# A second value/gate pair of a projection computed by seven block products, with moves of three kinds of work around it

## The chip, the cores and the metric

One core of one Trainium2 chip. The time is that of one execution in microseconds of device time, shown as the median of several runs; a profiled execution has a time of its own. The engines are TensorE (PE, with its weight loads PEld), VectorE (DVE), ScalarE (ACT), GpSimd (POOL) and SyncE (SP). SP, ACT and POOL can issue DMA transfers, each from a queue of its own, in order.

## The reference

One layer of a hybrid decoder trunk over 1024 positions of 1024 channels, in float32. Only the first half matters here:

```python
h = rms_norm(x, g_mix[l])
z = jnp.einsum("bsd,de->bse", h, w_in[l]) + b_in[l]
va, ga, xb, gb, sa, sb = jnp.split(z, cuts, axis=-1)      # 1024, 1024, 1536, 1536, 1024, 1024 channels
u = va * jax.nn.sigmoid(ga)
u = causal_depthwise_conv(u, conv_a_w[l], conv_a_b[l])    # width 31; then layer norm, silu, w_a_out -> y_a
v = causal_depthwise_conv(xb, conv_b_w[l], conv_b_b[l])   # width 4
v = rg_lru(v, ...)                                        # two gates by 16 heads of 96 x 96, then a scan
y_b = einsum(v * gelu(gb), w_b_out[l])
m = sigmoid(sa) * y_a + sigmoid(sb) * y_b                 # then w_o, residual, MLP of 4096, residual, norm
```

## The kernel before

Every float32 product is made of three matmuls on split operands: high part by high, high by low, low by high (`mm3`, `chunk_mm`, `z_mm`). A high part is a rounded copy by ACT. A low part is made either by DVE (a subtraction, function `split` or a `later` entry) or through POOL: `split_dma` (lines 63 to 68) lets ACT write the negated rounded value and a DMA issued by POOL add the source onto it.

The input projection has two stages.

**Chunks.** A chunk is 128 output channels over all 1024 positions. List `CH` (line 711) gives their order, three of them begun before the loop. A chunk takes 24 weight blocks by two halves of the positions, 48 matmuls (`chunk_mm`). In each slot of the loop (`for s in range(3, NC1)`) PE runs one chunk, with the two gate products of a head (`head_mm`, six matmuls each, into one PSUM buffer of the tag `ps2`) between its parts, in slots 4 to 23. ACT reads a head's bank with a sigmoid (`head_gate`, line 541); in every group of four heads, the third (head 2, 6, 10, 14) is spread over three tiles, by three row transfers per gate (line 546). After a group of four heads `scan_exp` (exponential and tanh), `scan_root` (square root), `scan_in` and `scan_tile` prepare and run the recurrence of three channel tiles. `VA+j` and `GA+j` are the value and gate chunks of channel tile j of branch A; `NJ` tiles go this way.

**Block products.** The other channels go in pairs of chunks (`ZPAIRS`), each by a Winograd form of Strassen's scheme: seven products of half-size blocks in place of eight. A product (i, p) is 12 matmuls into one PSUM bank (`z_mm`, line 948). `zseq` is the order of all products, a place each. At place n the loop also makes the left operand of place n + 4 (`z_lhs`), the sums of blocks for place n + 5 (`z_sums`), and the work after the products of places n - 1 and n - 2 (`z_post`, `z_post2`). `ZL` says at which place the weights of a pair are loaded, into four buffers of the tag `p`, and `ZX` holds further work by place. Right operands 4 to 7 are sums of blocks of the normed input: computed and stored early (`x_sum`, `x_make`, `x_store`), those in `RAW` unsplit, and fetched back (`x_get` for split parts, `x_raw` then `x_split` for raw ones). The pair `u7` is the last value/gate pair; `z_branch` puts it together.

**What fills DVE.** The width-31 convolution (`conv`) of each of the eight channel tiles of branch A is 48 steps on DVE. The planner keeps clocks of expected time (`clk`) for PE, ACT and DVE; `later` queues a DVE operation with a time when it is ready, `vector_work` emits the queue in that order, and `fill` puts convolution steps into the gaps. While `taps["hold"]` is set no new convolution begins. A convolution's result is stored (`yd`, line 661) and added up by POOL's DMA queue (`sum_up`); the sum is needed in the middle of the following stage, branch B's projection (`b_mm`, with `n_mean`).

Later stages (branch A's output projection `ga`, the projection `go`, the MLP's first products `gu` and `f`) have an order by places too (`gseq`, `GX`); `up_lhs` makes left operands of the MLP.

The order on each engine is the order in which these loops emit, and each engine and queue works in order.

Of the kernel before, what the change touches and what calls it, by code (L numbers as in the profile page):

```python
# [15 lines left out]
P = 128  # L16
# [5 lines left out]
HD = 96  # L22
# [9 lines left out]
def trunk_kernel(ctx: ExitStack, tc: tile.TileContext, x, xt_in, xt_eo, vecs, w_in, w_a_out, w_b_out,  # L32
                 w_rg, w_o, w_1, w_2, g_final, out):

    nc = tc.nc
# [458 lines left out]
    gate = {}  # L494
# [39 lines left out]
    def head_gate(n, gi, ready):  # L534
        g, hh = divmod(n, 4)
        tiles = [3 * g + WHOLE[hh]] if hh in WHOLE else range(3 * g, 3 * g + 3)
        for t in tiles:
            if (gi, t) not in gate:
                gate[gi, t] = T(f"g{gi}_{t}")
        a = gate[gi, tiles[0]][:HD] if hh in WHOLE else H(f"g{n}_{gi}", "g")  # L540
        nc.scalar.activation(a, gps.pop((n, gi))[:HD, :], AF.Sigmoid,  # L541
                             bias=(ba_c, bx_c)[gi][:, n:n + 1])
        at("A", 1.11, ready)
        if hh not in WHOLE:
            for ti, t in enumerate(tiles):
                nc.sync.dma_start(gate[gi, t][HD:P, :], a[32 * ti:32 * ti + 32, :])
# [163 lines left out]
    NJ = 7  # L710
    CH = [XB + 0, VA + 0, GA + 0, XB + 1, XB + 2, VA + 1, GA + 1, XB + 3, XB + 4, XB + 5, VA + 2, GA + 2, XB + 6, XB + 7, XB + 8, VA + 3, GA + 3, XB + 9, XB + 10, XB + 11, VA + 4, GA + 4, VA + 5, GA + 5, GA + 6, VA + 6]
    NC1 = len(CH)
# [25 lines left out]
    def chunk_mm(s, n0, n1, halves=(0, 1), low_last=False):  # L738
# [16 lines left out]
        for t in "s0 s1 g0 g1 g2 s2 s3 u7 g3 g4 g5 t0 t1 t2 t3".split()]  # L755
# [31 lines left out]
    def z_lhs(i, p):  # L787
        src = z_blk(i, *{1: (0, 0), 2: (0, 1), 4: (1, 1)}[p]) if p in (1, 2, 4) else \
            zs[i, {3: 4, 5: 1, 6: 2, 7: 3}[p]]
        zn[0] += 1  # L790
        o = (wp.tile([P, 2, 4, P], F32R, tag="w", name=f"zo{i}_{p}") if zn[0] % 5 > 2 or zn[0] % 5 == 0 else
             qp.tile([P, 2, 4, P], F32R, tag="g", name=f"zo{i}_{p}", bufs=2))
        if p in (7, 5) or conv_over():
            nc.scalar.activation(o[:, 0], src, AF.Copy)
            later(at("A", 0.6), 0.63, nc.vector.tensor_tensor, o[:, 1], src, o[:, 0].bitcast(F32),
                  ALU.subtract)
        else:
            split_dma(src, o[:, 0], o[:, 1])
            at("A", 1.15)
        zo[i, p] = o  # L800


    zseq = [(0, 1), (1, 1), (0, 2), (1, 2), (0, 6), (0, 7), (1, 7), (0, 5), (1, 6), (0, 3), (0, 4),
            (1, 5)]
    for i in range(2, NZ):
        zseq += [(i, 1), (i, 7), (i - 1, 4), (i, 6), (i, 2), (i - 1, 3), (i, 5)]
# [4 lines left out]
    for i in range(2, NZ):  # L811
        n = zseq.index((i, 1))
        ZL[n - 9] = ((z_load, i, 0),)
        ZL[n - (6 if i > 2 else 4)] = ((z_load, i, 1),)
    def z_get(n, f):
# [8 lines left out]
    RAW = (4, 5)  # L824
    XS = {4: ((x_sum, 0),), 5: ((x_make, 0, 5), (x_make, 0, 7)), 6: ((x_make, 0, 6), (x_make, 0, 4), (x_sum, 1)),
          7: tuple((x_make, 1, p) for p in (5, 7, 6, 4)),
          NC1 - 3: ((scan_exp, 3),), NC1 - 2: ((x_get, 0, 6), (x_get, 1, 6)),
          NC1 - 1: ((scan_in, 0, 9, 10, 11), (scan_root, 3), (x_get, 0, 7), (x_get, 1, 7))}
# [204 lines left out]
    def z_post2(i, p):  # L1033
# [3 lines left out]
        elif p == 4:  # L1037
            z_out(i, 1, 0, zb[i, "u"], "c")

    ZX = {0: ((x_raw, 0, 5), (x_raw, 1, 5)), 1: ((later, 0, 4.8, scan_tile, 9),), 2: ((x_split, 0, 5),), 3: ((x_split, 1, 5),),  # L1040
          4: ((later, 0, 4.8, scan_tile, 10), (x_raw, 0, 4), (x_raw, 1, 4)), 6: ((x_split, 0, 4),), 7: ((x_split, 1, 4),),
          9: ((later, 0, 4.8, scan_tile, 11),)}
    H_AT = {2: (0, 0), 5: (1, 1), 3: (0, 1), 4: (1, 0)}
    with tc.manual_schedule(engines=ENGINES):
# [40 lines left out]
        u_value(NJ - 1, zps[NC1 - 1])  # L1085
        vector_work(clk["V"])
        z_h(0, 0, 0)
        for n in range(len(zseq) + 2):
# [5 lines left out]
            taps["hold"] = n < 6  # L1094
# [598 lines left out]
    def g_get(n, f):  # L1693
# [34 lines left out]
        7: ((g_parts, "u", 5, 1), (up_lhs, 1, 5), (g_t, "u", 0, 3), (g_t, "u", 1, 3)),  # L1728
        9: ((g_parts, "u", 7, 0), (up_lhs, 0, 7)), 10: ((g_parts, "u", 7, 1), (up_lhs, 1, 7)),
# [463 lines left out]
```

## Time and profile before

| | us |
|---|---|
| median of 3 runs (1542.11 to 1543.1) | 1542.4 |
| the profiled execution's own time | 1542.07 |
| its span, first to last instruction | 1540.3 |
| granted TensorE clock, mean | 0.998 |
| DVE busy in the span | 1228.9 |
| ACT busy in the span | 911.2 |
| POOL busy in the span | 184.7 |

A line of the profile names an engine, a line of the kernel, the tile written and the tiles read, then times. "busy" is time in which an engine worked; the idle time before an instruction is put down to what released it. PEld is the weight load of TensorE, which runs beside its matmuls.

### The profile page before, as it was taken

How to read it: one execution, taken by the hardware profiler on the slowest of the kernel's cores; microseconds unless marked ns; L12 is line 12 of the kernel's file. 1: busy time of each engine (PE TensorE's matmuls, PEld its weight loads, DVE VectorE, ACT ScalarE, POOL GpSimd, SP SyncE). 2: the span in 40 equal slices, each digit the busy share in tenths (PEclk: the TensorE clock that was granted, in tenths of full speed). 3: DMA queues.
4: the chain of work that ended last, by engine and by line, in shares of the span. 5: the costliest groups of instructions: out<-in, count | busy, mean ns of one | idle time of the engine just before them, and what ended most of it. 6: DMA issues, size and time to landing. Idle time of an engine off the chain costs nothing.

```text
span 1540.3 us, 19049 instructions
## 1 busy us (share of the span) xinstructions
PE 1530.1 (99%) x6765; PEld 1258.2 (82%) x6765; DVE 1228.9 (80%) x1660; ACT 911.2 (59%) x1270; POOL 184.7 (12%) x221
## 2 busy tenths in 40 slices
PE   9999999999999999999999999999999999999998
PEld 7888888788888888888888887888888888888886
DVE  6999988989999998478568879765555558888897
ACT  6758576667676676435375777444444475555553
POOL 0000000012222221000022332000000011111110
PEclk9999999999999999999999999999999999999999
DMA  7575554699998888844579898523333779888852
GB/s 295 115 235 149 149 145 116 159 280 244 255 249 214 219 225 253 272 172 128 187 194 304 191 194 201 195 82 132 114 116 108 241 212 232 223 225 222 204 125 110
DMA packets 133504, 296.02 MB, mean 192 GB/s; under 512 B 20896, under 2 KB 38944, under 8 KB 133408
## 3 DMA queue, kind: packets, MB, share of 16 engines
q1 hardware_dynamic: 102016, 215.10, 41.5%
q0 software_dynamic: 30672, 77.35, 27.5%
q10 hardware_dynamic: 720, 2.36, 0.4%
q8 instruction: 53, 0.87, 0.2%
q14 instruction: 43, 0.35, 0.1%
HBM read 155.03 MB, written 60.82 MB: 140 GB/s over the span
## 4 chain that ended last, share of the span: by engine, by line
PE 97%; DMA 1%; ACT 1%; DVE 1%; issue 0%; SPq 0%; POOL 0%; DVEq 0%; POOLq 0%; ACTq 0%
PE z L749 16%; PE d L1946 15%; PE yb L1165 8%; PE e L2063 3%; PE keep L1946 2%; PE z L257 2%; PE rg L529 1%; PE rg L531 1%; PE rg L530 1%; DMA w_raw<-in_w_dram 1%; DMA xc<-in_xt_dram 0%; PE z4a L948 0%; PE go2e L1341 0%; PE z4e L948 0%; PE z2e L948 0%; PE z3e L948 0%
## 5 line engine op out<-in xcount | busy, mean ns | idle before, releaser
L749 PE MATMUL z<-xh,win_h 128*128 128x512 f32 x368 | 115.0, 390 | 0.0
L1958 DVE TENSOR_TENSOR acc<-acc,d 128x1024 f32<-128x1024 f32 x72 | 87.8, 1220 | 33.4 <-PE d L1946 32.7
L749 PE MATMUL z<-xl,win_h 128*128 128x512 f32 x368 | 113.5, 389 | 0.0
L749 PE MATMUL z<-xh,win_l 128*128 128x512 f32 x368 | 91.8, 391 | 0.0
L653 DVE SCALAR_TENSOR_TENSOR y<-u,vec,y 128x511 f32<-128x511 f32 (+14 forms) x120 | 88.4, 737 | 0.0
L653 DVE SCALAR_TENSOR_TENSOR y<-yt,csum,y 128x511 f32<-128x511 f32 (+6 forms) x112 | 82.6, 738 | 0.0
L653 DVE SCALAR_TENSOR_TENSOR yt<-u,vec,yt 128x511 f32<-128x511 f32 (+6 forms) x112 | 82.6, 737 | 0.0
L749 PEld LDWEIGHTS z<-xh,win_l 128*128 128x128 f32 x368 | 69.1, 188 | 15.6
L749 PEld LDWEIGHTS z<-xh,win_h 128*128 128x128 f32 x368 | 69.0, 188 | 15.3 <-ACT win_h L68 0.4
L541 ACT ACTIVATE g<-rg,vec 96x1024 f32<-96x1024 f32 x32 | 35.7, 1115 | 77.0 <-PE rg L531 76.3
L749 PEld LDWEIGHTS z<-xl,win_h 128*128 128x128 f32 x368 | 69.1, 188 | 14.6
L1623 ACT ACTIVATE o<-s 128x512 fp32r<-128x512 f32 x58 | 34.7, 624 | 54.6 <-DVE s L1608 24.5
L475 DVE SCALAR_TENSOR_TENSOR v<-xb,vec,v 128x1023 f32<-128x1023 f32 (+2 forms) x36 | 46.2, 1283 | 14.8 <-ACT v L466 13.9
L67 POOL DMA_DIRECT2D win_l<-win_raw x23 | 19.9, 867 | 306.9 <-ACT win_l L66 245.7
L67 POOL DMA_DIRECT2D zo<-zw x42 | 36.3, 863 | 130.6 <-ACT zo L66 108.0
L1165 PE MATMUL yb<-hgh,wb_h 128*128 128x512 f32 x168 | 51.7, 389 | 0.0
L1165 PE MATMUL yb<-hgl,wb_h 128*128 128x512 f32 x168 | 51.7, 389 | 0.0
L67 POOL DMA_DIRECT2D db_1l<-wr x7 | 6.1, 865 | 309.9 <-DMA wr<-in_w_dram 254.2
L1165 PE MATMUL yb<-hgh,wb_l 128*128 128x512 f32 x168 | 41.0, 389 | 0.0
L66 ACT ACTIVATE zo<-zw 128x512 fp32r<-128x512 f32 x42 | 26.3, 626 | 21.5 <-issue 6.6
L1129 DVE TENSOR_TENSOR o<-s,o 128x512 fp32r<-128x512 f32 x58 | 38.8, 683 | 0.0
L1172 DVE TENSOR_TENSOR sb<-yb,sb 128x512 f32<-128x512 f32 x16 | 10.3, 685 | 34.4 <-PE yb L1165 34.4
(1826 smaller groups left out, 4750.7 us busy)
## 6 DMA issues: line engine op xcount, KB each, us to landing
w_raw<-in_w_dram SPq DMA_DIRECT2D x36, 512.0 KB, 5.7
fr<-fd SPq DMA_DIRECT2D x32, 512.0 KB, 5.7
wr<-in_w_dram SPq DMA_DIRECT2D x32, 512.0 KB, 6.6
zw<-in_w_in_dram SPq DMA_DIRECT2D x30, 512.0 KB, 6.7
win_raw<-in_w_in_dram SPq DMA_DIRECT2D x23, 512.0 KB, 4.5
win_l<-win_raw POOLq DMA_DIRECT2D x23, 512.0 KB, 4.6
zo<-zw POOLq DMA_DIRECT2D x42, 256.0 KB, 5.9
gates<-zg SPq DMA_DIRECT2D x32, 256.0 KB, 3.8
```

The costliest lines, as they stand in the source:

```text
L67: nc.gpsimd.dma_start(l, src, accum_op=ALU.add)
L257: nc.tensor.matmul(z0[i][:, HALVES[hf]], w0[i][w][:, k, :], xpart(a, hf, k), start=k == 0 and which == "hh", stop=k == 7 and which == ("hl ...
L475: nc.vector.scalar_tensor_tensor(v[:, d:S], a[:, 0:S - d], cbw_c[:, w * 12 + t:w * 12 + t + 1], v[:, d:S], ALU.mult, ALU.add)
L541: nc.scalar.activation(a, gps.pop((n, gi))[:HD, :], AF.Sigmoid, bias=(ba_c, bx_c)[gi][:, n:n + 1])
L653: nc.vector.scalar_tensor_tensor(o[:, k:], a[:, 0:HS - k], c, o[:, k:], ALU.mult, add)
L749: nc.tensor.matmul(zps[s][:, HALVES[hf]], w[:, k, :], xw[k][part][hf], start=n == 0, stop=n == 23)
L1129: tt(l, src, h.bitcast(F32), ALU.subtract)
L1165: nc.tensor.matmul(ps[hf], a, b[:, HALVES[hf]], start=n == 0, stop=n == len(todo) - 1)
L1623: nc.scalar.activation(o[:, 0], src, AF.Copy)
L1946: nc.tensor.matmul(o, a, b, start=n == 0 and (p != 1 or g == 0), stop=n == len(todo) - 1, skip_group_check=p == 1 and g > 0)
L1958: tt(acc[p, q2], acc[p, q2], ps, ALU.add)
L2063: nc.tensor.matmul(o, a, b, start=n == 0 and t < 7, stop=n == len(todo) - 1, skip_group_check=t == 7)
```

## The change

- `NJ` goes from 7 to 6: chunks `GA+6` and `VA+6` leave `CH`, and the order of the last two becomes `GA+5`, `VA+5`. The pair `u6` enters `ZPAIRS` as the seventh of sixteen.
- The products of the first pairs are reordered: (0, 4) goes from place 10 to 15, (1, 4) from 14 to 16, (1, 5) from 11 to 10, (1, 3) from 17 to 13. Pair 3's first weights are loaded seven places ahead of its first product, not nine.
- Right operand 7 is now stored raw, fetched late and split at places 2 and 3; operand 5 is split at 4 and 5, operand 4 at 12 and 13. The last group's exponentials move into the slot of head 14's gates (two tiles) and place 0 (one), its square roots to place 5, its scans to places 6, 8 and 11.
- The first five left operands get their low parts from DVE, not through POOL.
- Head 14's six row transfers are issued by ACT, not SP.
- Holds on new convolutions: the last slot (before: the last three), and places 0 to 4 (before: 0 to 5).
- In the MLP's start `up_lhs` of (1, 5) moves from place 7 to place 9 of its list.

```diff
-                nc.sync.dma_start(gate[gi, t][HD:P, :], a[32 * ti:32 * ti + 32, :])
+                (nc.scalar if n > 11 else nc.sync).dma_start(gate[gi, t][HD:P, :], a[32 * ti:32 * ti + 32, :])
...
-    NJ = 7
+    NJ = 6
...
-        for t in "s0 s1 g0 g1 g2 s2 s3 u7 g3 g4 g5 t0 t1 t2 t3".split()]
+        for t in "s0 s1 g0 g1 g2 s2 u6 s3 g3 u7 g4 g5 t0 t1 t2 t3".split()]
...
-        if p in (7, 5) or conv_over():
+        if p in (7, 5) or zn[0] <= 5 or conv_over():
...
-    zseq = [(0, 1), (1, 1), (0, 2), (1, 2), (0, 6), (0, 7), (1, 7), (0, 5), (1, 6), (0, 3), (0, 4),
-            (1, 5)]
-    for i in range(2, NZ):
+    zseq = [(0, 1), (1, 1), (0, 2), (1, 2), (0, 6), (0, 7), (1, 7), (0, 5), (1, 6), (0, 3), (1, 5)]
+    zseq += [(2, 1), (2, 7), (1, 3), (2, 6), (0, 4), (1, 4), (2, 2), (2, 5)]
+    for i in range(3, NZ):
         zseq += [(i, 1), (i, 7), (i - 1, 4), (i, 6), (i, 2), (i - 1, 3), (i, 5)]
...
-        ZL[n - 9] = ((z_load, i, 0),)
+        ZL[n - (9 if i != 3 else 7)] = ((z_load, i, 0),)
...
-    RAW = (4, 5)
+    RAW = (4, 5, 7)
...
-          NC1 - 3: ((scan_exp, 3),), NC1 - 2: ((x_get, 0, 6), (x_get, 1, 6)),
-          NC1 - 1: ((scan_in, 0, 9, 10, 11), (scan_root, 3), (x_get, 0, 7), (x_get, 1, 7))}
+          NC1 - 2: ((scan_exp, 3, (0, 1)),),
+          NC1 - 1: ((x_get, 0, 6), (x_get, 1, 6), (x_raw, 0, 7), (x_raw, 1, 7), (scan_in, 0, 9, 10))}
...
-            taps["hold"] = s > NC1 - 4
+            taps["hold"] = s in range(23, 99)
...
-    ZX = {0: ((x_raw, 0, 5), (x_raw, 1, 5)), 1: ((later, 0, 4.8, scan_tile, 9),), 2: ((x_split, 0, 5),), 3: ((x_split, 1, 5),),
-          4: ((later, 0, 4.8, scan_tile, 10), (x_raw, 0, 4), (x_raw, 1, 4)), 6: ((x_split, 0, 4),), 7: ((x_split, 1, 4),),
-          9: ((later, 0, 4.8, scan_tile, 11),)}
+    ZX = {2: ((x_split, 0, 7),), 3: ((x_split, 1, 7),), 0: ((scan_exp, 3, (2,)),),
+          4: ((x_split, 0, 5),), 5: ((x_split, 1, 5), (scan_root, 3)),
+          6: ((later, 0, 4.8, scan_tile, 9),), 8: ((x_raw, 0, 4), (x_raw, 1, 4), (later, 0, 4.8, scan_tile, 10)),
+          12: ((x_split, 0, 4),),
+          13: ((x_split, 1, 4),), 11: ((later, 0, 4.8, scan_tile, 11),)}
...
         u_value(NJ - 1, zps[NC1 - 1])
+        scan_in(0, 11)
         vector_work(clk["V"])
+        x_raw(0, 5)
+        x_raw(1, 5)
...
-            taps["hold"] = n < 6
+            taps["hold"] = n in range(0, 5)
...
-        7: ((g_parts, "u", 5, 1), (up_lhs, 1, 5), (g_t, "u", 0, 3), (g_t, "u", 1, 3)),
-        9: ((g_parts, "u", 7, 0), (up_lhs, 0, 7)), 10: ((g_parts, "u", 7, 1), (up_lhs, 1, 7)),
+        7: ((g_parts, "u", 5, 1), (g_t, "u", 0, 3), (g_t, "u", 1, 3)),
+        9: ((up_lhs, 1, 5), (g_parts, "u", 7, 0), (up_lhs, 0, 7)), 10: ((g_parts, "u", 7, 1), (up_lhs, 1, 7)),
```

More of the change, by code (lines that the diff above doesn't have):

```diff
@@ L708, in x_split @@
               ALU.subtract)
-    NJ = 7
-    CH = [XB + 0, VA + 0, GA + 0, XB + 1, XB + 2, VA + 1, GA + 1, XB + 3, XB + 4, XB + 5, VA + 2, GA + 2, XB + 6, XB + 7, XB + 8, VA + 3, GA + 3, XB + 9, XB + 10, XB + 11, VA + 4, GA + 4, VA + 5, GA + 5, GA + 6, VA + 6]
+    NJ = 6
+    CH = [XB + 0, VA + 0, GA + 0, XB + 1, XB + 2, VA + 1, GA + 1, XB + 3, XB + 4, XB + 5, VA + 2, GA + 2, XB + 6, XB + 7, XB + 8, VA + 3, GA + 3, XB + 9, XB + 10, XB + 11, VA + 4, GA + 4, GA + 5, VA + 5]
     NC1 = len(CH)
```

## The prediction, as it was made

> **What bounds the kernel now.** I read the page first: the busy shares, then the chain that ended last. The reader is to see that TensorE (PE) is busy for 99% of the span and owns 97% of the chain, while every other engine has idle time.
>
> ```profile
> span 1540.3 us, 19049 instructions
> PE 1530.1 (99%) x6765; PEld 1258.2 (82%) x6765; DVE 1228.9 (80%) x1660; ACT 911.2 (59%) x1270; POOL 184.7 (12%) x221
> PE 97%; DMA 1%; ACT 1%; DVE 1%; issue 0%; SPq 0%; POOL 0%; DVEq 0%; POOLq 0%; ACTq 0%
> ```
>
> A share is a mean over stages, so next come the windows by stage: the end of the projections by chunks (314 to 339.2 us), and the block products (339.2 to 627). Columns: busy time with count of PE, weight loads, VectorE (DVE), ScalarE (ACT), GpSimd (POOL), granted clock, DMA share, GB/s.
>
> ```profile
> 314.00:339.20 25.20, 25.20 (x111) 20.49 (x110) 21.19 (x30) 22.80 (x25) 4.31 (x5) 1.00 0.91 301
> 339.20:627.00 287.80, 287.80 (x1270) 237.76 (x1269) 262.40 (x388) 195.65 (x320) 62.98 (x73) 1.00 0.91 239
> ```
>
> PE is busy all the time in both. But ACT around the changeover (22.80 of 25.20, 90%) and DVE in the products (91%) are nearly full, so they can take over if more is put on them. Third, all that PE waited for (in total, times, longest), and rows of the chain in order of time (start, length, what) from the chunks and the block products:
>
> ```profile
> PE spare L344 <- POOL ones L114: 1.6, 1, 1.6
> PE gu4a L1341 <- ACT u_late L1395: 0.6, 1, 0.6
> PE z L257 <- ACT xh L226: 0.4, 2, 0.2
> PE z L257 <- DVE xl L230: 0.2, 1, 0.2
> ```
>
> ```profile
> 305.00 8.18 PE z L749 x36
> 339.39 2.72 PE z0a L948 x12
> 624.43 2.72 PE z14f L948 x12
> ```
>
> All waits together are 2.8 us of 1540, and 1.6 of it is before the start of the work. So this kernel is a row of matmuls laid end to end: its time changes by the number of matmuls, plus any wait that a change makes or removes. A product of 12 matmuls takes 2.72 us, 0.2267 us each; 36 take 8.18, the same.
>
> **The change part by part.**
>
> *Matmuls.* A chunk is 24 pairs by two halves, 48 matmuls; chunks VA+6 and GA+6 go, 96 in all, 96 x 0.2267 = 21.76 us. The pair u6 comes in as seven products of 12: 84, 19.04 us. The difference is **-2.72 us**, all of it on the path. Nothing hides it, because PE waits for nobody in these stages.
>
> *One stall goes.* In the chunk stage of before one chunk started late, as its parts stood behind the exponentials on ACT:
>
> ```profile
> 324.43 3.79 PE L749 MATMUL z<-xh,win_l 128*128 128x512 f32 x16
> 328.21 0.73 PE L749 MATMUL z<-xh,win_h 128*128 128x512 f32 x2
> 328.79 0.62 PE L749 MATMUL z<-xl,win_h 128*128 128x512 f32 x2
> ```
>
> 16 x 0.2267 from 324.43 end at 328.06, and the next pair takes 0.73 instead of 0.62: 0.15 + 0.11 = 0.26 us. That chunk was VA+6; in the new kernel the last chunk's parts are made a slot earlier, ahead of the exponentials. **-0.26.**
>
> *ScalarE in the last two slots.* All slots up to 23 keep their place, and the products start at 339.39 - 21.76 - 0.26 = 317.4. What ACT did in two further slots has to fit ahead of that or behind it. The ACT rows of before:
>
> ```profile
> 300.88 1.11 ACT L541 ACTIVATE g<-rg,vec 96x1024 f32<-96x1024 f32 x1 [5.57 <-PE rg L531]
> 302.60 0.71 ACT L636 ACTIVATE yt<-u,vec 128x512 f32<-128x512 f32 x1
> 314.61 1.11 ACT L541 ACTIVATE g<-rg,vec 96x1024 f32<-96x1024 f32 x1 [6.57 <-PE rg L531]
> 315.74 1.28 ACT L556 ACT_TABLE_LOAD   x1
> 317.04 1.16 ACT L556 ACTIVATE a<-g,c 128x1024 f32<-128x1024 f32 x1
> 321.51 1.14 ACT L556 ACTIVATE a<-g,c 128x1024 f32<-128x1024 f32 x1
> ```
>
> ```profile
> L546 SPq DMA_DIRECT2D g<-g x24: 507/542/1143, 95.0 to 303.2; - x24
> L684 ACTq DMA_DIRECT2D xsd<-xs7h x2: 326/336/346, 79.3 to 105.5; - x2
> ```
>
> Behind head 14's second gate (300.88, done 302.0) ACT now also issues three row transfers, then loads the table for the exponentials of two tiles, runs them, and only then comes to the convolution's two copies and head 15's first gate, which needs the sigmoid's table back. Until that gate has read it, head 15's bank (tag ps2, one buffer) stays full, and PE wants it for the head's second product right behind the 36 matmuls of the chunk, at 305.00 + 8.18 = 313.2. This wait is new. Six row transfers on ACT's queue do not appear in before; bounds are 0.34 each (ACT's own issues) and 0.54 (the same rows on SP), with 1.14 the longest. I take 0.54, since that row is of the same shape. The first three fall into ACT's idle 5.57 us and cost nothing. Then: 302.0 + 3 x 0.57 with gaps = 303.7; table 1.30, 305.0; two tiles at 321.51 - 317.04 = 4.47, 309.5; two copies 0.71 each, 310.9; table 1.30, 312.2; gate 1.12, 313.3. PE is held for 0.1 and restarts 0.1 slower, as the late chunk above did; with as much again for the semaphores I take **+0.3** (0 with 0.34 per issue, 2.1 with 1.14). SP, for its part, is rid of the six rows (3.2 us) and gets to the first loads for the products that much sooner. What is late next: two high copies and their lows on DVE are wanted at 317.4 + 0.45 (the third matmul); ACT has them at 314.4, DVE at about 315.8, hidden with 2 us to spare. ACT's own remainder (gate of the values, head 15's second gate, two copies) ends near 317.5, where the products begin, so nothing is queued up.
>
> Here the Trainium skill speaks against the change. Its page "ScalarE: Activation LUTs", section "What ACT_TABLE_LOAD costs", counts a drain of about 1380 ns on top of a load of about 1283, 2.66 us for each switch. The trace disagrees: ACT is done at 315.72, the load runs 315.74 to 317.02 and the next function starts at 317.04. By the page the two new switches would hold PE for some 2.8 us more, an estimate.
>
> *Edits with one answer.* Rows of before, the first a window (columns as above):
>
> ```profile
> 339.40:366.60 27.20, 27.20 (x121) 22.52 (x121) 26.69 (x32) 19.15 (x30) 4.34 (x5) 1.00 0.88 229
> L452 DVE TENSOR_TENSOR zo<-zs,zo x33: 666/685/694, 348.0 to 610.9; 128x512 fp32r<-128x512 f32 x33
> 328.81 3.49 DVE L452 TENSOR_TENSOR g<-g,v 128x1024 f32<-128x1024 f32 x3
> ```
>
> Five lows on DVE instead of POOL: 5 x 0.69 = 3.4 us of DVE, five POOL issues less. DVE was full in the first ten products (26.69 of 27.20) and PE was never held. Into that stretch now come the lows, one product of the scan's input (3.49 / 3 = 1.16) and block 7's two lows of the same size; out of it go block 4's two lows, and the three scans are spread to places 6, 8 and 11. Hidden; if that cover is gone, the 3 us net are PE's. Block 7's raw store takes copies and issues from ACT and DVE in slots 5 to 7, off the path; its raw load is asked for by 314, with a flight of at most 11.5 (row below) it is there at 326, and ACT splits it at places 2 and 3 for place 5, 331. The rest of the new pair's work (four sums, lows, gates' products, some 8 us of DVE) goes into a stage with 16 us more of products than before.
>
> *Products 4 later.* (0,4) goes from place 10 to 15, (1,4) from 14 to 16, so the raw blocks of pairs 0 and 1 that they read are held until places 11 and 12 split them, and pair 3's blocks, which take those buffers, load later. Rows of before:
>
> ```profile
> 368.53 0.32 SPq L577 DMA_DIRECT2D hd<-g  x1
> 368.95 0.38 SPq L764 DMA_DIRECT2D zw<-in_w_in_dram  x1
> zo<-zw POOLq DMA_DIRECT2D x42, 256.0 KB, 5.9
> DMA to landing us min/median/max: 4.2/6.7/11.5
> ```
>
> (The last is that of the zw loads.) Place n starts at 317.4 + 2.72n. The split for (0,4) starts on ACT near 348.1; 0.6 later POOL can issue, and it lands 5.9 after: 354.6. SP has the store of the last scan tile ahead, done about then. Load 354.6, landing at 361.3. ACT wants it for (3,1) at place 15, 358.2, so ACT stands 3 us; (3,1) is split at 361.3 and lands at 367.8, wanted at place 19, 369.1 + 0.45. It decides from a flight of 8.5 us on: bounds 0 and 3.0 us of PE. I take **+0.2**.
>
> *Conversions in the MLP start.* up_lhs(1,5) moves behind two products. PE's 0.6 us wait for u_late stood behind its two copies, 1.0 us (the first of them and what follows):
>
> ```profile
> 946.31 0.62 ACT L66 ACTIVATE o<-s 128x512 fp32r<-128x512 f32 x1
> 947.83 0.58 ACT L1395 ACTIVATE u_late<-gu4a 128x512 f32<-128x512 f32 x1
> 949.85 0.63 ACT L66 ACTIVATE o<-s 128x512 fp32r<-128x512 f32 x1 [0.49 <-DVE s L1611]
> 950.90 0.58 ACT L1395 ACTIVATE u_late<-gu5a 128x512 f32<-128x512 f32 x1
> 951.54 3.01 PE gu5a L1341 x12
> ```
>
> The first u_late comes 1 us sooner. But the second hangs on DVE's s (949.85), which does not move, and gu5a started at 951.54 right behind it; PE only gets there sooner and waits there. Its POOL issue and low land some 1 us later than before, for a product wanted behind gu5a. Taken: **0** (bounds -1.0, both waits gone with their slow restarts, and +0.3).
>
> *Tail of the convolutions.* The last two channel tiles of branch A now come from places 53 and 74, 462 and 519 us, and their taps fill what DVE has left. Rows of before: the last convolution's store, the last add into ysum, and the split that needs it.
>
> ```profile
> L661 SPq DMA_DIRECT2D yd<-y x8: 320/364/1214, 128.9 to 595.7; - x8
> L614 POOL DMA_DIRECT2D ysum<-yd x7: 871/1225/1258, 409.8 to 598.8; - x7
> L1203 ACT ACTIVATE ysumh<-ysum x1: 1044/1044/1044, 642.4 to 642.4; 128x1024 fp32r<-128x1024 f32 x1
> ```
>
> Some 8 us more work on an engine that is 91% full, and 2.5 us less time up to there: 11 of the 43 us between 598.8 and 642.4. **0.**
>
> **Sum**: -2.72 - 0.26 + 0.3 + 0.2 + 0 = **-2.5 us**. The profiled execution took 1542.07 (span 1540.3 and 1.8 around it): 1539.6. The median shown is 0.3 above it, so I give **1539.9**.
>
> **The rivals.**
> A (forecast), 1539.3 to 1541: as above.
> B, every new wait is hidden and the MLP waits go: -2.72 - 0.26 - 1.0 = -4.0, so 1538.4 to 1539.3. For it: two of my waits are within 0.3 us of none. Against: gu5a hangs on DVE.
> C, ScalarE becomes the bound at head 15's bank: the three issues at 1.14 add 1.8 us, or each switch of table takes twice its 1.28 us, 2.6 more: 1541 to 1542.6. For it: ACT is full from 302 to 317. Against: the rows at 315.74 and 317.04, ACT's own issues of 0.34. The table rule has 0.03 of the chance (the skill's page above is where it stands).
> D, **slower**: pair 3's blocks come late. If both fly near the longest, 11.5, the first holds (3,1) by 3.0 us and the second, asked for at 358, lands at 369.5 where DVE wants it for its sums at place 17, 363.7; DVE then stands for 5.8 us, and behind it in order the adds that empty banks, taken as half of that for PE. -2.5 - 0.2 + 3.0 + 2.9 = +3.2, 1545.6; with the spread 1542.6 to 1547. It decides from a flight of 8.5 us on and is slower than before from about 11. Against: the median flight is 6.7.
> That the pair is not really cheaper is excluded: 84 matmuls against 96 is a count.
>
> **How the numbers follow.** Chances: A 0.40, B 0.27, C 0.15, D 0.18. A measurement of this kernel can tell about 0.2%, 3.1 us, from no change. Over 0.2% faster is below 1539.3, case B: 0.27. Over 0.2% slower is above 1545.5, most of D: 0.13. The rest, 0.60, lies within. Range 1538.2 to 1545.0: below B's end nothing, above it a little over D's 0.13.
>
> **What would show it.** PE count 6753; products from 317.7 to about 622.5; a PE wait for ACT g (L541) near 313 of 0 to 0.5 us; no slow pair in the last chunk; ACT standing some 3 us for zw near 358; gu5a with the wait that gu4a had; last yd store near 595. The prediction is wrong if PE waits for zo's lows at places 0 to 10, if any PE wait is over 1 us, or if the product's 2.72 us changes.

## The result, and the profile after

| | before | after |
|---|---|---|
| median of the runs side by side, us | 1542.75 (1542.11 to 1543.65, 4 runs) | 1556.34 (1553.12 to 1557.4, 4 runs) |
| ratio after to before, 95% interval | | 1.0084 (1.0067 to 1.0102) |
| profiled execution, its span | 1542.07, 1540.3 | 1553.12, 1551.3 |

In what follows the *rows* are head 14's six row transfers, *lefts* are left operands of the block products, *lows* their low parts, *raw blocks* the stored right operands that are split late, and a *bank* is the PSUM buffer that a product or a gate is added up in. "After" is the changed kernel.

The change makes the kernel 13.6 us slower; 1539.9 was forecast, with a range up to 1545.0. The profiled execution of after is the fastest of its four, so its trace holds 11.0 us of the difference, not 13.6.

First the page of after: span, busy times, and the chain by engine.

```profile
span 1551.3 us, 19074 instructions
PE 1531.0 (99%) x6753; PEld 1257.0 (81%) x6753; DVE 1234.4 (80%) x1668; ACT 924.3 (60%) x1291; POOL 188.0 (12%) x225
PE 91%; DMA 4%; issue 2%; DVE 1%; ACT 1%; SPq 0%; POOL 0%; DVEq 0%; POOLq 0%
```

The 12 matmuls fewer are there (6765 to 6753). DVE and ACT do 5 and 13 us more, nothing that a span of 1551 could not hold. But PE's share of the chain falls from 97 to 91%, and DMA, DVE and ACT come in: the row of matmuls now has holes. All that PE waited for in after (in total, times, longest):

```profile
PE z0a L948 <- ACT z0b L1014: 3.5, 1, 3.5
PE yb L1170 <- ACT hgh L1070: 1.7, 1, 1.7
PE spare L344 <- POOL ones L114: 1.6, 1, 1.6
PE gu4a L1346 <- ACT u_late L1400: 1.2, 1, 1.2
PE z0f L948 <- DVE xb4l L452: 1.1, 2, 0.7
PE z2e L948 <- DMA zo<-zs: 0.7, 1, 0.7
...
PE rg L529 <- ACT g L541: 0.3, 1, 0.3
```

A wait also makes the next matmuls slower (the first distance behind one is mostly 0.34 us), so I count holes by the starts of successive matmuls: the sum of what each distance has beyond 0.227 us, of the distances over 0.245 and from 45 us on. That gives 2.16 us in before and 16.18 in after, 14.0 more; less 2.72 for the 12 matmuls it is 11.3, and the spans differ by 11.0. The holes account for the whole loss. By place: head 15's bank at 313.0, 0.59; place 2 of the block products at 326.5, 5.35; places 13 to 30 (358 to 410 us), 4.64; one at 524, 0.50; the start of the second projection (644 to 646), 2.80; gu4a and gu5a 1.84 (1.17 before).

How the largest came about is read on three engines. DVE, then ACT, then PE of after (start, length, what, and in brackets the idle time before it with what ended it):

```profile
303.67 0.75 DVE L653 SCALAR_TENSOR_TENSOR y<-yt,csum,y 128x510 f32<-128x510 f32 x1
307.99 2.36 DVE L452 TENSOR_TENSOR g<-g,v 128x1024 f32<-128x1024 f32 x2 [3.57 <-DMA g<-g]
...
315.11 1.27 DVE L452 TENSOR_TENSOR zo<-zw,zo 128x512 fp32r<-128x512 f32 x2
316.30 0.74 DVE L653 SCALAR_TENSOR_TENSOR yt<-u,vec,yt 128x510 f32<-128x510 f32 x1
...
320.25 0.69 DVE L452 TENSOR_TENSOR zs<-zw,zw 128x512 f32<-128x512 f32 x1
```

```profile
301.48 3.13 ACTq L546 DMA_DIRECT2D g<-g  x3
...
321.70 0.63 ACT L794 ACTIVATE zo<-zs 128x512 fp32r<-128x512 f32 x1 [4.69 <-DVE zs L452]
322.35 1.28 ACT L556 ACT_TABLE_LOAD   x1
323.65 1.15 ACT L556 ACTIVATE a<-g,c 128x1024 f32<-128x1024 f32 x1
324.83 1.15 ACT L557 ACTIVATE g<-g,sm 128x1024 f32<-128x1024 f32 x1
325.88 0.58 ACT L1014 ACTIVATE z0b<-z0a 128x512 f32<-128x512 f32 x1
```

```profile
326.51 0.79 PE L948 MATMUL z0a<-xh,zo 128*128 128x512 f32 x1 [3.50 <-ACT z0b L1014]
327.11 0.63 PE L948 MATMUL z0a<-xl,zo 128*128 128x512 f32 x1
327.53 1.05 PE L948 MATMUL z0a<-xh,zo 128*128 128x512 f32 x2
```

DVE stood 3.57 us for head 14's rows and fell behind; after the lows of two lefts (315.11) it still took six steps of a convolution, and so the first sums (zs) began at 320.25, and ACT, which had ended its own list at 317.0, stood 4.69 us for them, being in order; behind them stood the exponential of tile 11 with its table load, 3.63 us, and only then the copy of product 1 into the next bank, which product 2 adds to. PE waited 3.5 us for that copy, and then ran its next matmuls 0.426 us apart instead of 0.227.

How late the rows were (those of head 14's second gate; after, then before: issues with shortest, median and longest time, then the flight):

```profile
L546 ACTq DMA_DIRECT2D g<-g x3: 514/764/1721, 301.5 to 302.9; - x3
...
DMA to landing us min/median/max: 6.5/6.6/6.8
```

```profile
L546 SPq DMA_DIRECT2D g<-g x3: 507/582/583, 302.0 to 303.2; - x3
...
DMA to landing us min/median/max: 2.2/2.3/2.4
```

They were issued half a microsecond sooner and landed four later. SP, rid of them, had sent two 512 KB loads of the first blocks at 300.1 and 300.6 and a 512 KB store at 301.1, ahead of the rows, and another store at 301.6, among them. That these make the flight long is what the traces offer; it was not tried alone. They also show that the queue by itself doesn't. The rows of head 14's first gate go by ACT too, in after with two such loads in flight (they landed at 293.4 and 296.6), and in e7 (below: the kernel before with rows by ACT) with one that landed at 292.9; after, then e7:

```profile
L546 ACTq DMA_DIRECT2D g<-g x3: 546/597/599, 291.9 to 293.2; - x3
...
DMA to landing us min/median/max: 5.1/5.3/5.3
```

```profile
L546 ACTq DMA_DIRECT2D g<-g x3: 594/602/607, 292.3 to 293.5; - x3
...
DMA to landing us min/median/max: 2.3/2.3/2.4
```

Two queues don't give two sets of transfer engines: the Trainium skill, "DMA: Bandwidth & Descriptors", section "Issuing engines are not separate DMA queues", says that transfers of all issuers interleave on the same 16 engines and only the issuer's time is saved. The traces agree: on ACT's queue the rows flew 5.3 and 6.6 us beside SP's transfers, and 2.3 us where there was hardly one.

### The profile page after: what moved, and what is told of

It reads as the page before. It is cut to its first block, busy times and chain, and to the rows that moved or that the text cites. A ratio compares the mean times of both kernels' runs of the same rounds, so it can differ in the third digit from the quotient of the medians.

```text
span 1551.3 us, 19074 instructions
## 1 busy us (share of the span) xinstructions
PE 1531.0 (99%) x6753; PEld 1257.0 (81%) x6753; DVE 1234.4 (80%) x1668; ACT 924.3 (60%) x1291; POOL 188.0 (12%) x225
## 4 chain that ended last, share of the span: by engine, by line
PE 91%; DMA 4%; issue 2%; DVE 1%; ACT 1%; SPq 0%; POOL 0%; DVEq 0%; POOLq 0%
PE d L1951 15%; PE z L749 14%; PE yb L1170 8%; PE e L2068 3%; PE keep L1951 2%; PE z L257 2%; DMA hg<-hgd 1%; DMA zo<-zw 1%; PE rg L531 1%; PE rg L529 1%; PE rg L530 1%; DMA zo<-zs 1%; DMA xb7l<-xsd 0%; DMA g<-g 0%; PE gu5a L1346 0%
## 5 line engine op out<-in xcount | busy, mean ns | idle before, releaser
L749 PE MATMUL z<-xh,win_h 128*128 128x512 f32 x336 | 105.1, 390 | 0.0
L749 PE MATMUL z<-xl,win_h 128*128 128x512 f32 x336 | 103.7, 389 | 0.0
L749 PE MATMUL z<-xh,win_l 128*128 128x512 f32 x336 | 84.2, 391 | 0.0
L749 PEld LDWEIGHTS z<-xh,win_l 128*128 128x128 f32 x336 | 63.1, 188 | 14.3
L749 PEld LDWEIGHTS z<-xh,win_h 128*128 128x128 f32 x336 | 63.1, 188 | 13.7
L749 PEld LDWEIGHTS z<-xl,win_h 128*128 128x128 f32 x336 | 63.1, 188 | 13.3
L67 POOL DMA_DIRECT2D zo<-zs x31 | 26.9, 868 | 122.3 <-ACT zo L66 114.2
```

The costliest lines, as they stand in the source:

```text
L67: nc.gpsimd.dma_start(l, src, accum_op=ALU.add)
L749: nc.tensor.matmul(zps[s][:, HALVES[hf]], w[:, k, :], xw[k][part][hf], start=n == 0, stop=n == 23)
```

## The experiments

Each run was made beside the kernel before. "us" is the median, then the ratio to before with its interval.

| run | edit | us | ratio |
|---|---|---|---|
| e1_exp_place3 | after, exponential of tile 11 at place 3 | 1558.21 | 1.0106 (1.0092 to 1.0120) |
| e2_rows_sync | after, rows by SP | 1549.04 | 1.0042 (1.0028 to 1.0055) |
| e3_lows_pool | after, first lefts' lows through POOL | 1554.48 | 1.0073 (1.0058 to 1.0088) |
| b1_mlp_move | before, up_lhs moved | 1542.24 | 1.0000 (0.9991 to 1.0009) |
| e5_scans_later | e2, two scans later | 1545.98 | 1.0023 (1.0013 to 1.0033) |
| e6_products4_early | e2, products 4 early again, a scan one place earlier | 1551.73 | 1.0061 (1.0045 to 1.0076) |
| e7_before_rows_act | before, rows by ACT | 1542.93 | 1.0003 (0.9993 to 1.0012) |
| e8_rows_sync_lows_pool | e2 and e3 | 1555.03 | 1.0082 (1.0067 to 1.0097) |
| e9_scans_exp_later | e5, exponential at place 3 | 1549.54 | 1.0044 (1.0029 to 1.0060) |
| e10_candidate | e9, three more edits | 1545.81 | 1.0026 (1.0016 to 1.0035) |
| e11_no_sum_at_tail | e2, no change of order | 1549.67 | 1.0044 (1.0030 to 1.0058) |
| e12_candidate_exp0 | e10, exponential at place 0 | 1543.61 | 1.0010 (1.0001 to 1.0018) |
| e13_candidate_exp1 | e10, exponential at place 1 | 1544.39 | 1.0014 (1.0005 to 1.0023) |
| e14_no_last_sum | e2 without the last sum | 1549.67 | 1.0050 (1.0032 to 1.0069) |
| e15_exp_ahead | e12, exponential ahead of place 0 | 1543.53 | 1.0008 (0.9999 to 1.0016) |
| e16_exp_ahead_lows6 | e15, two more lows by DVE | 1543.29 | 1.0004 (0.9995 to 1.0013) |

My theory after the result was the chain above, with the rows as its first link; the rivals were that only ACT's order at place 2 is wrong, that DVE's new lows are too much, and that DVE is late whatever is moved.

**Single parts.** e1: the exponential leaves place 0.

```diff
-    ZX = {2: ((x_split, 0, 7),), 3: ((x_split, 1, 7),), 0: ((scan_exp, 3, (2,)),),
+    ZX = {2: ((x_split, 0, 7),), 3: ((x_split, 1, 7), (scan_exp, 3, (2,))),
```

> The changed kernel with the exponential of the last tile moved from place 0 to place 3. Theory (ScalarE's order): the copy into bank z0b stands in ScalarE's queue behind this exponential, 3.6 us; without it the 3.5 us wait of PE for that copy at 326.5 falls below 0.7 us and the half-rate matmuls behind it go: about 5 us faster than the changed kernel, 1551 us. Rival (VectorE is simply late): the sums that ScalarE waits for come at 321.7 in any case, so the copy moves from 325.9 to 322.9 at best and the delay turns up again at the later places: under 2 us faster.

It did not get faster; both the theory and the rival had it faster. PE's wait for the copy fell to 0.4 us, but right behind it PE waited 1.7 for a low part from DVE, and then at places 7 to 10 (340 to 352 us, 3.7 us of holes) for the split of block 5 and for copies. The holes at 644 are gone in this trace, but 4.2 us came at 632 to 640, behind a zc sum (a sum on DVE after the products). DVE was late, and ACT's order only hid it.

e2: all rows go out by SP again.

```diff
-                (nc.scalar if n > 11 else nc.sync).dma_start(gate[gi, t][HD:P, :], a[32 * ti:32 * ti + 32, :])
+                nc.sync.dma_start(gate[gi, t][HD:P, :], a[32 * ti:32 * ti + 32, :])
```

> The changed kernel with head 14's rows issued by SyncE again. Theory (ScalarE's order alone): ScalarE gets 3.1 us back ahead of head 15's gate, so the 0.3 us wait for its bank goes, but the wait at place 2 stays above 2.5 us: 1 us faster at most, 1555 us. Rival (the rows' queue): the rows landed 6.5 us after their issue and VectorE stood 3.57 us for them; on SyncE they land after 2.3 us, VectorE's sums come 3.5 us sooner, the wait at place 2 and most of the waits up to place 25 go: 6 to 9 us faster than the changed kernel, 1547 to 1550 us.

This is the largest single part. What PE waits for in e2 (rows as above):

```profile
PE z1f L948 <- DMA zo<-zw: 1.2, 1, 1.2
PE yb L1170 <- ACT hgh L1070: 1.0, 1, 1.0
PE z0a L948 <- ACT z0b L1014: 1.0, 1, 1.0
```

The wait at head 15's bank is gone, DVE goes from its convolution straight to the gate products, and the hole at place 2 falls from 5.35 to 1.25 us. The first sum, ACT's wait for it and the copy into the next bank are now:

```profile
317.27 0.68 DVE L452 TENSOR_TENSOR zs<-zw,zw 128x512 f32<-128x512 f32 x1
```

```profile
318.71 0.63 ACT L794 ACTIVATE zo<-zs 128x512 fp32r<-128x512 f32 x1 [2.40 <-DVE zs L452]
...
322.90 0.57 ACT L1014 ACTIVATE z0b<-z0a 128x512 f32<-128x512 f32 x1
```

The edit does two things: the rows land sooner, and ACT has its 3.13 us of issues back. For place 2 the first is what counts, for ACT stands and waits for the sums here too, and sum and copy both come 2.98 us sooner. Not all of it stays: the holes from 354 to 412 us grow from 4.6 to 6.7. By medians the rows are worth 7.3 us, by the ratios 6.5; the two profiled executions differ by 3.7 (1553.12 and 1549.41), so part of it is in runs without a trace. Two of the other three runs of after had a mean granted clock of 0.996, where the profiled one and all of e2 have 0.998 or more.

e7 is the counterpart: the same rows by ACT in the kernel before.

> The kernel before (1542 us) with nothing but head 14's rows issued from ScalarE. Theory (ScalarE's queue hurts through what waits for the rows, and in the kernel before the products of gate and value come only in the last slot, so that the rows have time): 1541.8 to 1543 us, with the stall at head 15's bank (0.3 to 0.6 us) alone. Rival (3.1 us of ScalarE and later rows cost the same wherever they are): 1547 us or more.

No difference, though the flight of the second gate's rows was 5.0 us (median of three) there too. A row of its DVE tells why:

```profile
328.62 2.35 DVE L452 TENSOR_TENSOR g<-g,v 128x1024 f32<-128x1024 f32 x2
```

The last row landed at 308.4, and the products of gate and value, which read them, come 20 us later; in after DVE was ready for them at 304.4. So, within that interval (1.9 us at most), late rows cost only what waits for them.

e3 and e8 (with SP's rows):

```diff
-        if p in (7, 5) or zn[0] <= 5 or conv_over():
+        if p in (7, 5) or conv_over():
```

> The changed kernel with the first lefts' low parts through GpSimd's queue again. Theory (ScalarE's order): five more copies of 0.5 us on ScalarE make place 2 later, VectorE wins 3.4 us: within 2 us of the changed kernel. Rival (VectorE overloaded): VectorE's 3.4 us are what is missing, the sums come at 320 instead of 321.7 and the waits shrink: 3 to 5 us faster than the changed kernel.

> The changed kernel with rows by SyncE and with the low parts of the first lefts by GpSimd's accumulating transfer again; what is left of the change is the second pair by block products, the order with products 4 later, and the moved up_lhs. If the two costs add (7.3 and 1.9 us in the runs that undid one): 1547 to 1547.5 us. If they share one cause, VectorE behind at the changeover: 1548 to 1549.5 us. If the low parts by GpSimd land late once the rest is early (they land 6 to 8 us after issue): above 1549.5 us.

With rows by ACT the lows on DVE cost 1.9 us by the medians, but the intervals of the two ratios overlap; with rows by SP they save 6.0 (1555.03 against 1549.04): through POOL the first low lands late (PE stands 1.3 us for it at 319.0), and the waits for blocks 7 and 5 come besides. The parts don't add, and this part of the change helps.

e6 puts products 4 back at places 10 and 14.

```diff
-    zseq = [..., (0, 3), (1, 5)]
-    zseq += [(2, 1), (2, 7), (1, 3), (2, 6), (0, 4), (1, 4), (2, 2), (2, 5)]
+    zseq = [..., (0, 3), (0, 4), (1, 5)]
+    zseq += [(2, 1), (2, 7), (1, 4), (2, 6), (2, 2), (1, 3), (2, 5)]
...
-        ZL[n - (9 if i != 3 else 7)] = ((z_load, i, 0),)
+        ZL[n - 9] = ((z_load, i, 0),)
...
-          6: ((later, 0, 4.8, scan_tile, 9),), 8: ((x_raw, 0, 4), (x_raw, 1, 4), (later, 0, 4.8, scan_tile, 10)),
-          12: ((x_split, 0, 4),),
-          13: ((x_split, 1, 4),), 11: ((later, 0, 4.8, scan_tile, 11),)}
+          6: ((later, 0, 4.8, scan_tile, 9), (x_raw, 0, 4), (x_raw, 1, 4)), 7: ((later, 0, 4.8, scan_tile, 10),),
+          8: ((x_split, 0, 4),), 9: ((x_split, 1, 4),), 11: ((later, 0, 4.8, scan_tile, 11),)}
```

> The changed kernel with SyncE rows (1549.0 us) and products 4 of the first two pairs back at places 10 and 14, pair 3's first blocks loaded nine places ahead again, x_raw of products 4 at place 6 and its splits at 8 and 9. Theory (the move of products 4 is a remedy, not a cost): their rights can't be there by place 10, since VectorE is in its scans, so PE waits some 5 us or more there: 1552 us or more. Rival (the later products 4 and the pair 3 blocks loaded two places later cause the waits of 355 to 407 us, 5.8 us together): 1544 to 1547 us.

It is 2.7 us slower than e2 by the medians (the intervals just overlap), where rival D, with pair 3's blocks, would have had it faster. But the run doesn't settle this, since its edit also moves the scan of tile 10 from place 8 to 7. PE waited 3.6 us in one piece for the zc sum, which stood behind that scan on DVE, and the product then ran at half speed (DVE, then PE):

```profile
344.96 2.29 DVE L576 TENSOR_TENSOR_SCAN g<-a,g 128x1024 f32<-128x1024 f32 x1
...
348.35 0.68 DVE L452 TENSOR_TENSOR zc<-zc,z0f 128x512 f32<-128x512 f32 x1
```

```profile
349.18 0.77 PE L948 MATMUL z0f<-xb4h,zo 128*128 128x512 f32 x1 [3.60 <-DVE zc L452]
```

These holes, 6.8 us from 345 to 355, are new; those behind them up to 412 us, 6.7 in e2, fell to 2.1.

b1, in the kernel before:

```diff
-        7: ((g_parts, "u", 5, 1), (up_lhs, 1, 5), ...
-        9: ((g_parts, ...
+        7: ((g_parts, "u", 5, 1), ...
+        9: ((up_lhs, 1, 5), (g_parts, ...
```

> The kernel before with the one move in the MLP's start, nothing else. Prediction on record: no change, the first wait (u_late of gu4a, 0.6 us) goes over to gu5a: within 0.3 us of the kernel before. Rival: both waits go, 1.0 us faster. Second rival, from the trace of the changed kernel (gu4a waited 1.2 us there): the move itself makes it 0.5 to 1 us slower.

No change in time, as forecast, but not by the way that was forecast. u_late came only 0.3 us sooner (947.50 against 947.83), and PE stood for it 0.9 sooner, since four matmuls of f1b now come behind gu4a's product instead of ahead of it. So gu4a's wait grew from 0.6 to 1.2 us, where it was to go over to gu5a.

**What is left in e2.** Its DVE, and its ACT, around places 8 to 14:

```profile
346.17 2.29 DVE L576 TENSOR_TENSOR_SCAN g<-a,g 128x1024 f32<-128x1024 f32 x1
348.38 0.66 DVE L452 TENSOR_TENSOR zc<-zc,z0f 128x512 f32<-128x512 f32 x1
...
353.52 2.29 DVE L576 TENSOR_TENSOR_SCAN g<-a,g 128x1024 f32<-128x1024 f32 x1
355.73 0.66 DVE L452 TENSOR_TENSOR zc<-zc,z1f 128x512 f32<-128x512 f32 x1
359.20 1.23 DVE L452 TENSOR_TENSOR xb4l<-xb4l,xb4h 128x1024 fp32r<-128x1024 f32 x1 [2.81 <-ACT xb4h L706]
```

```profile
349.07 0.76 ACT L973 ACTIVATE zg<-zc,vec 128x512 f32<-128x512 f32 x1 [2.43 <-DVE zc L452]
...
356.42 0.76 ACT L973 ACTIVATE zg<-zc,vec 128x512 f32<-128x512 f32 x1 [1.93 <-DVE zc L452]
```

Three scans stand in one stretch of DVE (the first at 340.1), the last two each ahead of a zc sum; ACT stands for those sums (2.43 and 1.93 us), and so the split of block 4 (its low on DVE at 359.2) and lefts for later pairs come late. Then DVE stands 2.8 us for ACT: two engines in order, each waiting for the other in turn. e5 moves two scans (entries of `ZX`, the others left out):

```diff
-          ... 8: (..., (later, 0, 4.8, scan_tile, 10)), ... 11: ((later, 0, 4.8, scan_tile, 11),)}
+          ... 15: ((later, 0, 4.8, scan_tile, 10),), 19: ((later, 0, 4.8, scan_tile, 11),)}
```

> The changed kernel with head 14's rows issued by SyncE again (1549.0 us, the run before this one), and besides with the scan of tile 10 moved from place 8 to 15 and that of tile 11 from place 11 to 19. Theory (VectorE does three scans of 4.8 us in one stretch from 337 to 355 us, ScalarE waits in order for the zc sums behind them, so the lows of products 4 and pair 2's and 3's lefts come late: 354.9 to 365.6 us, 3.0 us of PE waits): those waits go, and less of the later ones: 1545 to 1547 us. Rival (VectorE simply has more work than time from 310 us on, and what is moved comes back later): the waits move to 370 to 410 us, 1548.5 to 1550.5 us.

By the medians 3.1 us, in the theory's range, but its mechanism is only half there. The holes from 354 to 366 us fell from 3.35 to 0.59, as it said. Yet 1.4 at 377 is new, a zc sum behind the moved scan, and the two at 388 and 406 grew from 2.3 to 4.3: most of what went came back later, as the rival said, and up to 412 us only 0.4 us were won. What makes the trace of e5 2.3 us shorter is above all that the holes at 641 us, 2.06 in e2, are gone, which the theory had not named (more on them below).

e9 puts the exponential at place 3 (the edit of e1) on top of e5; e10 besides moves scan 11 one place on, begins the sums into ysum at place 26 instead of 20, and has up_lhs at its old step; e12 and e13 are e10 with the exponential at places 0 and 1. ysum is the tile into which POOL's queue adds up the convolutions. e10 against e9, beside up_lhs:

```diff
-          ... 19: ((later, 0, 4.8, scan_tile, 11),)}
+          ... 20: ((later, 0, 4.8, scan_tile, 11),)}
...
-            if n >= 20 and n % 6 == 2:
+            if n >= 26 and n % 6 == 2:
                 sum_up(clk["P"], 1)
```

> The run with SyncE rows and the scans of tiles 10 and 11 at places 15 and 19 (1546.0 us), and the exponential of tile 11 at place 3 instead of 0. Theory (at place 2 PE waits 1.0 us for the copy of product 1 behind that exponential and its table load, and nothing else of the changeover is late any more): that wait and its slow matmul go, 1.5 us, so 1544 to 1545 us. Rival (VectorE has no time anywhere up to place 10, as when the same move was made with ScalarE rows): a wait on a low part or on the next bank takes its place, 1545.5 to 1547 us.

> As the run with the exponential at place 3, and besides: the scan of tile 11 at place 20 instead of 19, so that pair 2's zc sum stands ahead of it; the sums of the convolutions into ysum from place 26 instead of 20; up_lhs(1, 5) back at its step of the kernel before. Theory (what is left of the waits at 377, 388 and 406 us, 5.1 us together, is the zc sum behind the scan and the low parts' transfers beside two 512 KB sums by the same GpSimd queue): 1539.5 to 1542 us, the 12 matmuls' 2.7 us at last a gain. Rival (the DMA share of 1.05 from 380 to 420 us is full whatever is in it): the waits move to 390 to 430 us, 1543.5 to 1546 us.

> The run that took four edits together (SyncE rows, scans 10 and 11 at places 15 and 20, sums into ysum from place 26, up_lhs(1, 5) at its old step), but with the exponential of tile 11 back at place 0. Theory (moving the exponential to place 3 only sent its 3.6 us of ScalarE to places 8 to 13, where they cost 3.5 us; the other edits took away the waits at 377, 388 and 406 us): 1541 to 1543 us. Rival (the other edits bring nothing, and the difference between those two runs is the up_lhs and noise): 1545 to 1546.5 us.

> The same with the exponential of tile 11 at place 1, behind the copy of product 1 into the next bank for pair 1 and ahead of that for pair 2. Theory (only the order of that copy and the exponential is wrong at place 0): the wait at 323.5 us (1.0 us and a slow matmul) goes and none comes: 1539.5 to 1541.5 us. Rival (the exponential has no free place before 350 us): a wait for the second copy or for the splits of products 7 and 5 takes its place, 1542.5 to 1546 us.

e9: the rival, and worse than it: the wait at place 2 went, and five came from 336 to 348, with a stretch at half clock at 393. By the medians the three edits bring 3.7 us (e10 against e9) and 2.4 (e12 against e5); which of the three is not separated (b1 gives up_lhs nothing). In e12 the holes from 375 to 410 are 1.3 us, 5.6 in e5. e10 and e13 came out in the range of their rivals, e12 0.6 us above that of its theory. Place 1 is no better than place 0.

e15 issues the exponential in front of the loop, into the 2.6 us in which ACT waited for the sums; e16 also has DVE make product 6's lows of pairs 2 and 3 (the second edit).

```diff
         z_get(3, z_lhs)
+        scan_exp(3, (2,))
...
-        if p in (7, 5) or zn[0] <= 5 or conv_over():
+        if p in (7, 5) or zn[0] <= 5 or (p == 6 and i in (2, 3)) or conv_over():
```

> As the run with four edits and the exponential at place 0 (1543.6 us), but with that exponential ahead of the copies of the first sums, where ScalarE waited 2.4 us for VectorE (316.3 to 318.7 us). Theory (the wait at place 2 is only ScalarE's order: 3.6 us of exponential between a sum that comes at 318.7 and the copy of product 1): the wait of 1.2 us and its slow matmul go and nothing takes their place: 1541.6 to 1542.6 us, no slower than the kernel before. Rival (the changeover has no slack: the sums' copies, now 1.1 us later, hold the lefts of products 6 and 7): waits of 1 us or more from 326 to 345 us, 1543.2 to 1545 us.

> The same, and the low parts of product 6's lefts of pairs 2 and 3 by VectorE instead of GpSimd's accumulating transfer. Theory (the waits at 357 and 380 us, 0.85 us together, are that transfer's flight of 6 to 9 us): they go, 1540.6 to 1542 us, under the kernel before. Rival (VectorE's 1.3 us more put off what stands behind): no better than the run beside it, or waits on zc or the next lows in their place.

The wait at place 2 did go in e15, but the total stayed: its trace has 1.1 us at 380 and 1.1 at 383 that e12 had at 0.5 and 0.1. In e16 these shrink, and 4.76 us of holes are left against 2.16 in before: 2.6 more, about the 2.7 that the matmuls save. That trace is of one of its faster runs (1541.58, the median is 1543.29). Both medians lie above the range of their theory, and neither run is faster than before; the interval of e16 begins at 0.9995. The largest waits left there are that of gu4a, 1.3 us, and one for a left of pair 3, 0.7 us.

**The holes at 644 us.** e11 was to take the last sum into ysum out of their way, but the order of every engine's instructions came out the same as in e2: it is a repetition of e2, 1549.67 beside 1549.04. e14 leaves that sum out.

```diff
-            if n >= 20 and n % 6 == 2:
+            if n in range(20, len(zseq) - 10) and n % 6 == 2:
...
-        summed.append((clk["V"] + 9, j))
+        done.append(j)
+        if len(done) < 8:
+            summed.append((clk["V"] + 9, j))
```

> The changed kernel with SyncE rows (1549.0 us), with no sum of a convolution into ysum in the last 10 places of the block products (the last one then comes with the second projection's first steps). Theory (conv 7 ends 29 us later than in the kernel before, and its sum, 512 KB from 630.4 to 638.0 us, runs beside the load of the last hg tile, whose flight is 6.5 us against 4.6 before): the waits at 641 and 642 us (1.85 us) go or shrink to below 0.5 us: 1547.3 to 1548.2 us. Rival (the load is issued late because the places before are late, whatever runs beside it): the waits stay, 1548.7 to 1549.6 us.

> The changed kernel with SyncE rows (1549.0 us), without the sum of the last convolution into ysum (the mean that is made of it lacks one of eight tiles; all else is computed). Theory (that sum, 512 KB from 630.4 to 638.0 us, makes the flight of the last hg load 6.5 us instead of 4.6): the two waits at 641 and 642 us go or shrink to below 0.6 us together: 1547.2 to 1548.2 us. Rival (other transfers of those 8 us do, or the load is issued late): 1.2 us or more of waits stay, 1548.4 to 1549.8 us.

The rival: without the sum the last load of hg (what branch B's projection, the second one, reads) still flew 6.6 us, and PE's waits of 1.0 and 0.5 us stayed. This is read from the trace, since the four runs of e14 spread from 1545.6 to 1554.3. ACT of after at the last load, and the flights of the last two hg loads in after and in e5:

```profile
643.55 1.06 ACT L1070 ACTIVATE hgh<-hg 128x1024 fp32r<-128x1024 f32 x1 [4.73 <-DMA hg<-hgd]
```

```profile
DMA to landing us min/median/max: 5.9/6.7/7.5
```

```profile
DMA to landing us min/median/max: 4.6/5.0/5.4
```

In after, e2 and e14 the last store of a convolution (512 KB) goes out at 624 to 628 us, among these loads, and PE waits. In before it went at 595.7, in e5 and e12 at 642.3 and 638.1, behind the last load, and PE doesn't wait. That the convolution ends late is thus not the cause, for in e5 it ends later still; that the store meets the loads fits all of these, but was not tried alone, and the load is also issued some 3 us later against PE's first product of this stage in after and e2 (8.7 and 9.0 us behind it, 5.9 in before, 7.7 in e5). This stays open.

## Why the prediction was wrong, step by step

- *Matmuls, -2.72*: right. PE has 6753 matmuls, and a product takes 2.72 us where nothing is waited for. *One stall goes, -0.26*: right, there is no late pair in the last chunk.
- *Head 15's bank, +0.3*: right in mechanism, 0.59 measured. The three issues took 3.13 us (0.51, 0.76 and 1.72), where 1.71 was summed and 1.14 was the longest bound. No drain shows behind the table loads: in after the load at 322.35 lasts 1.28 and the next function starts 0.02 behind it. Rival C's waits of 1 us and more at this bank did not come.
- ***"ACT's own remainder ... ends near 317.5, where the products begin, so nothing is queued up": the step that failed first.*** ACT did end its own list at 317.0; what failed is "nothing is queued up". I priced the rows at what they take to issue and never asked when they land and who reads them. That SP "gets to the first loads for the products that much sooner" I took for a gain, and it is these transfers beside which the rows flew 6.6 us; DVE's 3.57 us stand is not in the sum. And I ended the account of ACT at the first product: behind the two lefts' copies the list of place 0 has the exponential, 3.6 us, and behind it the copy that product 2 needs. The two halves of the path cross: rows late, DVE late, sums late, ACT standing, exponential, copy. Place 2 alone cost 5.35 us of holes; the whole of the rows' move 6.5 to 7.3.
- ***"Hidden; if that cover is gone, the 3 us net are PE's"***: failed too. Not by the lows, which were done in time (316.4, forecast 315.8, wanted at 317.6) and save time where the rows go by SP (e8), but by their company: the cover was DVE's convolution steps, and these are not put off when DVE is late, since the planner's clock, not the engine's, places them. In after six of them ran from 316.3 to 320.2 while ACT waited for the sums behind, and in e2 the same six from 313.3 to 317.2; what they cost was not tried alone. The same order of emission put the scans ahead of the zc sums (3.35 us of holes from 354 to 366 in e2).
- *Products 4 later, +0.2, and rival D*: too small, and the forecast cause is not what the traces show. There are 4.64 us of holes from 358 to 410, where 0.2 was summed and rival D had 5.9. That they lie there is no proof of D: in e12, with products 4 just as late, the holes from 354 to 412 are 1.9 us (6.7 in e2), so the late products alone need not cost them, and the order of scans and sums has the larger part. e6, which was to undo the move, also moved a scan and leaves its own price open. The 2.43 and 1.93 us for which ACT stands near 349 and 356 in e2 are for zc, not for pair 3's loads.
- *Conversions in the MLP start, 0*: the time is right (b1: 1.0000, 0.9991 to 1.0009), the working isn't: the first u_late came 0.3 us sooner, not 1, and gu4a's wait grew. The zero is in part luck.
- *Tail of the convolutions, 0*: wrong in kind. I compared the last store with the split that needs its sum, 43 us later, and it had that time. It went out at 627.1 instead of 595.7, in part since the changeover gave DVE fewer steps of the convolutions (below, before then after), and among the hg loads something cost 2.8 us; what, is open. The windows below count the convolutions' multiply-adds alone.

```profile
300.00:340.00 40.00, 23.19 (x35) 1.00 0.87 273
```

```profile
300.00:340.00 40.00, 10.23 (x15) 0.96 0.62 215
```

There are twenty steps fewer in these 40 us, at 0.66 each some 13 us of the 31; the rest was not traced.

Of the signs that would prove it wrong one came in after, a PE wait over 1 us, three times (3.5, 1.7 and 1.2; the 1.6 at the very start is in before too). The forecast that the pair itself is cheaper is not refuted: four edits of order bring the changed kernel to 1.0010 and six to 1.0004 (0.9995 to 1.0013). But the 2.7 us were not seen as a gain in the median of any run, and whether an order exists that gives them is open.

## What to carry to other kernels

Where one engine owns 97% of the chain, the gain of fewer instructions is counted in a minute; the risk is at the stage's border, and there each engine's list has to be walked past the first instruction that is wanted, up to the first few places of the next stage. When a transfer changes its queue, ask first what the freed queue will send ahead of it and who reads what lands late: the same six rows cost nothing where their reader came 20 us later and some 7 us where it came at once. And parts of one change don't add: undo them singly and in pairs before one is blamed, and see that an undo moves nothing else.

## What the hardware showed unexpectedly

After some holds PE ran at half its clock for some 3 us. Windows of after: the hold, the 3.5 us behind it, and the next (the column after the busy times is the granted clock).

```profile
322.80:326.50 3.70, 0.21 (x1) 0.00 (x0) 3.70 (x6) 3.65 (x5) 0.00 (x0) 1.00 0.44 142
326.50:330.00 3.50, 3.49 (x8) 2.80 (x9) 3.43 (x5) 3.48 (x5) 0.00 (x0) 0.51 0.00 0
330.00:333.50 3.50, 3.50 (x17) 2.85 (x16) 2.39 (x5) 2.44 (x4) 0.00 (x0) 1.00 0.10 34
```

Starts are 0.426 us apart where 0.227 is usual; it made the hold of 3.5 us cost 5.35. The Trainium skill, "TensorE: Matmul & The Clock Gate", section "Part 1: The HAM clock gate (the "warmup" mystery)", has the clock halved after an idle window of about 3.4 us and 426.7 ns per matmul of this size then; the measured distance agrees. The length does not quite: e6 shows it after 3.6 us, but e14 after a hold of 1.95 us, from 0.6 us behind the restart on, and e9 after one of 2.2 us, there only from 1.6 us behind the restart on:

```profile
391.40:393.00 1.60, 1.60 (x6) 1.28 (x7) 0.69 (x1) 0.06 (x1) 0.00 (x0) 0.92 1.07 294
393.00:396.20 3.20, 3.20 (x9) 2.55 (x8) 1.87 (x3) 2.91 (x6) 0.85 (x1) 0.51 1.04 383
```

e5 had a hold of 2.2 us without it. So a hold of 2 us may cost some 1.5 us more or nothing, and what decides between them is not settled here.
